# Two of the weight sums of the MLPs' seven products made by GpSimd in halves, the first one issued one unit sooner

## The chip, the core and the metric

The kernel runs on one core of one Trainium2 chip. Its engines are TensorE (PE in the profile; its weight loads are PEld), VectorE (DVE), ScalarE (ACT), GpSimd (POOL) and SyncE (SP, which here only issues DMAs). Each runs its own queue of instructions in order, and semaphores tie the queues together. The metric is the time of one execution on the device, in microseconds (us), as the median of some runs.

## The reference

A trunk of two decoder layers over 256 tokens of width 2048, all in float32. The first layer's mixer is differential attention, the second's multi-head latent attention. Each layer then attends into 256 memory tokens and ends with an MLP whose hidden width is 8192:

```python
def sq_relu_mlp(h, wup, wdown):
    return jnp.square(jax.nn.relu(h @ wup)) @ wdown

x = x + sq_relu_mlp(rms_norm(x, mlp_norm[i]), mlp_wup[i], mlp_wdown[i])
```

The change touches only the product `h @ wup` of the two MLPs: 256 x 2048 times 2048 x 8192.

## The kernel before, in words

**Precision.** A float32 product is made as three products of halves. Activations and weights are each split into a high part (fp32r) and a low part, the rest; TensorE adds high x high, high x low and low x high. For the weights this is done on the fly. A raw tile of 128 x 2048 float32 (1 MB, one "unit" of the weight stream) comes by DMA; for each of its two halves of 1024 columns ScalarE casts the high part (`whi`, L223) and VectorE subtracts to get the low part (`wlo`, L224: raw minus whi, both in SBUF). There are seven raw tiles (pool `wraw`) and four tiles each of whi and wlo (pool `whalf`), so the split can be at most two units ahead of TensorE.

**Weight stream.** `plan` lists the units in the order of use. `take()` hands TensorE the next unit and refills a list of four ready ones through `fill()`. `fill()` pops a job; before it runs that job, it calls the `fetch` of the job behind it, if it has one. So a fetch is issued one unit ahead of its job's split. SyncE's loads and the accumulating DMAs are kept in program order; TensorE's order is written out by hand. The order of the other instructions of VectorE, ScalarE and GpSimd is chosen by a scheduler that works from its own estimates of times and from dependencies.

**Seven products.** The hidden width is taken in eight blocks of 1024. Blocks 1 to 7 are computed by a scheme of seven products in place of eight (class `Seven`): tokens, width and hidden columns are each cut in two, and sums of the quarters of activations and weights are multiplied (p1 to p7). Each product has two units, x = 0 and 1, of 12 matmuls of 512 columns. The order is p1 p1 p5 p5 p6 p3 p6 p3 p2 p7 p2 p7 p4 p4. Wdown units of earlier blocks (24 matmuls each) are woven in behind seven of these: p1(1), p5(1), both p6, both p2, p7(1).

**Weight sums.** For each x a tile `t` holds a running sum. It is loaded with one quarter. Behind p1 a second quarter is added on the way by an accumulating DMA that GpSimd issues (L961); p5 uses that sum. For p6 the quarter in tile `22` is added to `t` by VectorE (`add`, L969), for p2 the quarter in tile `21` likewise (L969 again, called at L1000); the result is p4's weight. p3 uses tile `22`, behind which another accumulating DMA makes it p7's weight. p6's sum is issued in the job itself, right ahead of its split; it must wait until p5 of the same x has split `t`, and until tile `22` has landed. In the first four of the seven blocks `t` for x = 0 lives in a unit of the activations' pool, which the profile shows as `unit`; otherwise it is a raw tile.

Other work that matters here: L616 adds a finished Wdown chunk to the residual (VectorE, one operand in PSUM); L428 splits transposed hidden activations (VectorE, both operands in SBUF); L394 stores planes for a transpose by DMA (issued by GpSimd). Elsewhere GpSimd makes small products and sums for the rotary embedding (L632 to L637) and two gains at the very end (L1896).

Of the kernel before, what the change touches and what calls it, by code (L numbers as in the profile page):

```python
# [15 lines left out]
ALU = mybir.AluOpType  # L16
# [6 lines left out]
CH = 512  # L23
# [31 lines left out]
def trunk(ctx, tc, x, xT, xT0, mem, memT, positions, gcols, gfinal, lam_vecs, consts, W, out):  # L55
    nc = tc.nc
# [20 lines left out]
    def unit():  # L77
        return units.tile([P, 2, 4, S], F32R, tag="unit", name=nm("unit"))
# [99 lines left out]
    def f32(ap):  # L178
        return ap.bitcast(F32)
# [47 lines left out]
    def halves_of(raw, n=4 * CH, pieces=2):  # L227
        split = split_pieces(raw, n, pieces)
        for _ in range(pieces):
            split.next()  # L230
        return split.halves
# [18 lines left out]
    def fill():  # L250
        while len(ready) < AHEAD and plan:
            job = plan.pop(0)
            if plan and hasattr(plan[0], "fetch"):
                plan[0].fetch()
            if callable(job):
                ready.append(job())
            else:
                name, i, width = job
                ready.append(split_weights(W[name][i, :, : 4 * width], width))
# [685 lines left out]
    class Seven:  # L945
# [20 lines left out]

        def job(self, p, x):
            def add(o, q):
                nc.vector.tensor_tensor(o, o, q, ALU.add)  # L969

            loads = {"p1": (("t", x), (0, 1)), "p6": ((22, x), (1, 1)), "p2": ((21, x), (1, 0))}

            def fetch():
                key, (i, j) = loads[p]
                if key not in self.raw:
                    home = f32(unit()).rearrange("p a k t -> p (a k t)") if p == "p1" and x == 0 and self.b < LAST - 2 else None
                    self.raw[key] = self.fetch(i, j, x, home=home)

            def run():
                r = self.raw  # L980
                if p in loads:
                    fetch()
                if p == "p1":
                    o = self.fetch(0, 0, x)
                    self.fetch(0, 0, x, r["t", x])
                elif p == "p5":
                    o = r["t", x]
                elif p == "p6":
                    o = r["t", x]
                    add(o, r[22, x])  # L990
                elif p == "p3":
                    o = r[22, x]
                    split = halves_of(o)
                    self.fetch(0, 1, x, o)
                    return split
                elif p == "p7":
                    o = r.pop((22, x))
                elif p == "p2":
                    o = r.pop((21, x))
                    add(r["t", x], o)  # L1000
                else:
                    o = r.pop(("t", x))
                return halves_of(o)

            if p in loads:
                run.fetch = fetch
            return run
# [997 lines left out]
```

## Time and profile before

| | |
|---|---|
| median of 3 runs | 2160.42 us (2160.02 to 2160.5) |
| the profiled execution's own time | 2159.85 us |
| its span | 2158.1 us |
| TensorE busy | 2147.1 us (99%) |
| VectorE busy | 1733.3 us (80%) |
| ScalarE busy | 1486.7 us (69%) |
| GpSimd busy | 225.4 us (10%) |
| weight sums on VectorE (L969) | 56 times 2.288 us |

The span reaches from the first to the last instruction of the profiled execution; the time holds some 1.75 us more. Busy means that an instruction of the engine was running; for TensorE the ends are modelled. In the answers on groups, the columns are the line, the engine, the operation, out<-in by tile names, the shapes, the count, busy time and the mean of one in ns, and the idle time ahead of it with what ended it. In a timeline, each row has its start, its duration (of several merged rows, from the first start to the last end) and in brackets the idle time ahead. In the table by stretches, busy times stand with the count of instructions, then the granted clock, the DMA engines' share and GB/s.

### The profile page before, as it was taken

Reading aid. Unit: us, or ns where it says so; the run is one execution under the profiler, and the core shown is the slowest. Engines: PE = TensorE matmul, PEld = TensorE weight load, DVE = VectorE, ACT = ScalarE, POOL = GpSimd, SP = SyncE. Lnnn points to the kernel's source line nnn. Section 1 sums busy time; section 2 is a strip of 40 time slices with the busy share of each in tenths; the row PEclk is TensorE's granted clock in tenths of the full one; section 3 lists DMA queues with packets and bytes.
Section 4 is the critical chain, followed back from the end, with each engine's and each line's share of the span. In section 5 each row is a group of like instructions: output and inputs, shape, how many; then the busy total and the mean of one; then the engine's idle time right before and its main releaser. Section 6 shows DMA issues by size and latency. Waiting matters only on the chain.

```text
span 2158.1 us, 27532 instructions
## 1 busy us (share of the span) xinstructions
PE 2147.1 (99%) x10109; PEld 1796.9 (83%) x10109; DVE 1733.3 (80%) x1962; ACT 1486.7 (69%) x1978; POOL 225.4 (10%) x354
## 2 busy tenths in 40 slices
PE   9999999999999999999999999999999999999998
PEld 7888888888888888888889988888888888888887
DVE  6576878788888889788886878778888888888887
ACT  7576656767777777776665765666777777777665
POOL 1123210001000000000000420000000000000001
PEclk9999999999999999999999999999999999999999
DMA  9678796748999999998986464665999999999995
GB/s 386 207 232 282 226 296 220 234 156 267 295 292 259 312 283 254 318 277 265 305 250 217 135 202 159 225 220 179 289 295 290 266 308 285 268 279 309 261 315 146
DMA packets 173944, 553.72 MB, mean 257 GB/s; under 512 B 100464, under 2 KB 100848, under 8 KB 114928
## 3 DMA queue, kind: packets, MB, share of 16 engines
q1 hardware_dynamic: 155136, 445.26, 58.6%
q0 software_dynamic: 18240, 105.92, 23.2%
q8 instruction: 79, 1.29, 0.2%
q10 hardware_dynamic: 432, 0.79, 0.1%
q14 instruction: 57, 0.47, 0.1%
HBM read 505.38 MB, written 24.12 MB: 245 GB/s over the span
## 4 chain that ended last, share of the span: by engine, by line
PE 96%; DVE 2%; DMA 1%; issue 1%; ACT 0%; DVEq 0%; POOLq 0%; POOL 0%
PE mm L172 63%; PE pr L172 28%; PE ax L172 3%; DMA raw<-in_mlp_wup_dram 1%; PE ax L176 1%; DVE wlo L224 1%; PE mm L176 1%; DVE raw L969 0%; DVE x L616 0%; DVE unit L428 0%; ACT whi L223 0%; PE ax L1326 0%; PE pr L176 0%; DVE unit L382 0%; DVE x L1875 0%
## 5 line engine op out<-in xcount | busy, mean ns | idle before, releaser
L224 DVE TENSOR_TENSOR wlo<-raw,whi 128x1024 fp32r<-128x1024 f32 (+3 forms) x930 | 1118.8, 1216 | 321.2 <-ACT whi L223 299.1
L223 ACT CAST whi<-raw 128x1024 fp32r<-128x1024 f32 (+3 forms) x929 | 968.2, 1044 | 541.6 <-PE mm L172 381.1
L172 PE MATMUL mm<-whi,unit 128*128 128x512 f32 (+2 forms) x4000 | 1268.9, 389 | 0.3
L172 PEld LDWEIGHTS mm<-whi,unit 128*128 128x128 f32 x4000 | 749.0, 188 | 148.9 <-DVE unit L382 1.1
L172 PE MATMUL mm<-wlo,unit 128*128 128x512 f32 (+2 forms) x2000 | 773.8, 387 | 0.2
L172 PE MATMUL pr<-whi,unit 128*128 128x512 f32 x1912 | 610.0, 389 | 0.0
L172 PEld LDWEIGHTS mm<-wlo,unit 128*128 128x128 f32 x2000 | 376.3, 188 | 73.6 <-DVE wlo L224 3.2
L172 PEld LDWEIGHTS pr<-whi,unit 128*128 128x128 f32 x1912 | 358.6, 188 | 73.4
L172 PE MATMUL pr<-wlo,unit 128*128 128x512 f32 x956 | 371.8, 389 | 0.4 <-DVE wlo L224 0.4
L172 PEld LDWEIGHTS pr<-wlo,unit 128*128 128x128 f32 x956 | 179.5, 188 | 39.2 <-DVE wlo L224 2.4
L394 POOL DMA_DIRECT2D turned<-planes x84 | 47.6, 567 | 732.2 <-ACT planes L392 706.6
L969 DVE TENSOR_TENSOR raw<-raw,raw 128x2048 f32<-128x2048 f32 x40 | 91.5, 2288 | 9.0 <-DMA raw<-in_mlp_wup_dram 8.8
L616 DVE TENSOR_TENSOR x<-x,mm 128x512 f32<-128x512 f32 x128 | 85.2, 682 | 15.2 <-PE mm L172 15.1
L961 POOL DMA_DIRECT2D raw<-in_mlp_wup_dram x48 | 43.4, 905 | 448.0 <-DVE wlo L224 425.7
L468 POOL TENSOR_TENSOR rs<-rs,mhalf 128x1 f32<-128x1 f32 (+1 forms) x26 | 21.7, 837 | 385.7 <-DVE rs L467 385.6
L224 DVE TENSOR_TENSOR wlo<-unit,whi 128x1024 fp32r<-128x1024 f32 x48 | 57.3, 1221 | 5.3 <-ACT whi L223 4.0
L223 ACT CAST whi<-unit 128x1024 fp32r<-128x1024 f32 x48 | 49.8, 1054 | 9.8 <-PE pr L172 9.8
L392 ACT COPY planes<-p 128x1024 uint16<-128x1024 uint16 x48 | 50.0, 1041 | 0.3
L172 PE MATMUL mm<-unit,whi 128*128 128x256 f32 x256 | 46.7, 284 | 0.0
L462 ACT ACTIVATE junk<-x 128x512 bf16<-128x512 f32 (+1 forms) x57 | 35.3, 619 | 11.0 <-DVE x L1174 5.2
L1539 ACT ACTIVATE p<-p,r 128x512 f32<-128x512 f32 x42 | 30.4, 724 | 15.3 <-DVE p L1044 7.4
L172 PEld LDWEIGHTS mm<-unit,whi 128*128 128x128 f32 x256 | 40.2, 192 | 0.3
(207 smaller groups left out, 1314.3 us busy)
## 6 DMA issues: line engine op xcount, KB each, us to landing
raw<-in_mlp_wdown_dram SPq DMA_DIRECT2D x128, 1024.0 KB, 7.2
raw<-in_mlp_wup_dram SPq DMA_DIRECT2D x120, 1024.0 KB, 7.0
raw<-in_mlp_wup_dram POOLq DMA_DIRECT2D x48, 1024.0 KB, 9.0
raw<-in_da_wqkv_dram SPq DMA_DIRECT2D x45, 1024.0 KB, 8.6
turned<-planes POOLq DMA_DIRECT2D x84, 256.0 KB, 6.1
raw<-in_da_wo_dram SPq DMA_DIRECT2D x16, 1024.0 KB, 8.2
raw<-in_ca_wkv_dram SPq DMA_DIRECT2D x16, 1024.0 KB, 7.6
raw<-in_mlp_wdown_dram POOLq DMA_DIRECT2D x16, 1024.0 KB, 10.2
```

The source lines that it names most:

```text
L172: return nc.tensor.matmul(o, stationary, moving, start=start, stop=stop, skip_group_check=onto)
L176: nc.tensor.transpose(o, src, ident)
L223: nc.scalar.copy(hi, r)
L224: nc.vector.tensor_tensor(lo, r, f32(hi), ALU.subtract)
L392: nc.scalar.copy(planes, src.bitcast(U16).rearrange("p (w s) -> p s w", s=2))
L394: nc.gpsimd.dma_start(there.rearrange("(q s) w -> q s w", s=2), planes)
L462: return nc.scalar.activation(junk[:, : src.shape[1]], src, AF.Square, scale=scale, accum_out=acc)
L468: nc.gpsimd.tensor_tensor(r[:, :n], r[:, :n], mhalf.broadcast_to([P, n]), ALU.pow)
L616: nc.vector.tensor_tensor(xc, xc, ps, ALU.add)
L961: tc.keep_in_program_order(nc.gpsimd.dma_start(onto, src, accum_op=ALU.add))
L969: nc.vector.tensor_tensor(o, o, q, ALU.add)
L1539: nc.scalar.activation(r, src, AF.Relu, scale=rstd[t])
```

## The change

The sum is made by GpSimd, as two instructions of 128 x 1024 rather than one of 128 x 2048. The sum for p6 is issued in `fetch`, one unit ahead of p6's own split; the sum for p2 stays in its job.

```diff
         def job(self, p, x):
             def add(o, q):
-                nc.vector.tensor_tensor(o, o, q, ALU.add)
+                for at in (slice(0, 2 * CH), slice(2 * CH, 4 * CH)):
+                    nc.gpsimd.tensor_tensor(o[:, at], o[:, at], q[:, at], ALU.add)
...
                     self.raw[key] = self.fetch(i, j, x, home=home)
+                    if p == "p6":
+                        add(self.raw["t", x], self.raw[22, x])
...
                 elif p == "p6":
                     o = r["t", x]
-                    add(o, r[22, x])
                 elif p == "p3":
```

## The prediction

> **What bounds the kernel now.** I read the page first: the busy shares, the chain of work that ended last, and the costliest groups; then who waited for whom; then one steady stretch of an MLP.
>
> ```profile
> PE 2147.1 (99%) x10109; PEld 1796.9 (83%) x10109; DVE 1733.3 (80%) x1962; ACT 1486.7 (69%) x1978; POOL 225.4 (10%) x354
> PE 96%; DVE 2%; DMA 1%; issue 1%; ACT 0%; DVEq 0%; POOLq 0%; POOL 0%
> L224 DVE TENSOR_TENSOR wlo<-raw,whi 128x1024 fp32r<-128x1024 f32 (+3 forms) x930 | 1118.8, 1216 | 321.2 <-ACT whi L223 299.1
> L969 DVE TENSOR_TENSOR raw<-raw,raw 128x2048 f32<-128x2048 f32 x40 | 91.5, 2288 | 9.0 <-DMA raw<-in_mlp_wup_dram 8.8
> ```
>
> TensorE is busy 99% of the span and is 96% of the chain. VectorE has 20% idle time, most of it ahead of the low-half subtraction (L224), where it waits for ScalarE. The sums to be moved are L969. Most of them write a raw tile, the rest a unit that serves as one:
>
> ```profile
> L969 DVE TENSOR_TENSOR unit<-unit,raw 128x2048 f32<-128x2048 f32 x16 | 36.6, 2288 | 0.8 <-DMA raw<-in_mlp_wup_dram 0.6
> PEld mm L172 <- DVE wlo L224: 3.2, 8, 0.5
> PEld pr L172 <- DVE wlo L224: 2.4, 5, 0.6
> ```
>
> So there are 56 sums, four in each of 14 blocks (seven per layer), and 128.1 us of VectorE work. The last two rows are the whole stake on the good side: TensorE's weight loads waited 5.6 us for VectorE's low halves in the entire run. More than about 6 us can't be won.
>
> One block of seven products with its woven Wdown items, from 653.80 to 730.00, is my sample; the next one begins where it ends. The chain of waits inside it:
>
> ```profile
> 664.68 5.44 PE mm L172 x24
> 670.12 5.44 PE pr L172 x24
> 675.56 5.44 PE mm L172 x24
> 681.00 2.72 PE pr L172 x12
> 683.73 5.44 PE mm L172 x24
> 689.16 5.44 PE pr L172 x24
> 694.61 5.44 PE mm L172 x24
> 700.04 5.44 PE pr L172 x24
> 705.48 5.44 PE mm L172 x24
> ```
>
> Every piece follows the one before without a gap: 24 matmuls in 5.44 us. A product unit (pr) lasts 2.72 us, a Wdown unit (mm) 5.44. By the order in the code the pieces are: Wdown; p5(0), p5(1); Wdown D1; p6(0); Wdown D2; p3(0), p6(1); Wdown D3; p3(1), p2(0); Wdown D4. Each unit comes in two halves, so I know when TensorE needs each low half: p6(0) at 681.00 and 682.36, and so on. The engines over the block, then L224 alone, then L969 alone:
>
> ```profile
> 653.80:730.00 76.20, 76.20 (x338) 63.10 (x337) 64.02 (x56) 55.81 (x61) 5.87 (x9) 1.00 0.97 292
> 653.80:730.00 76.20, 49.95 (x42) 1.00 0.97 292
> 653.80:730.00 76.20, 9.15 (x4) 1.00 0.97 292
> ```
>
> TensorE 76.20 of 76.20; VectorE 64.02, of which the sums are 9.15 and the subtractions 49.95; GpSimd 5.87.
>
> **What VectorE does around the sums**, in time:
>
> ```profile
> 665.25 2.36 DVE L224 TENSOR_TENSOR wlo<-unit,whi 128x1024 fp32r<-128x1024 f32 x2 [0.67 <-ACT whi L223]
> 667.64 2.29 DVE L969 TENSOR_TENSOR unit<-unit,raw 128x2048 f32<-128x2048 f32 x1
> 669.85 1.22 DVE L224 TENSOR_TENSOR wlo<-raw,whi 128x1024 fp32r<-128x1024 f32 x1
> 670.99 1.28 DVE L616 TENSOR_TENSOR x<-x,mm 128x512 f32<-128x512 f32 x2
> 696.52 2.36 DVE L224 TENSOR_TENSOR wlo<-raw,whi 128x1024 fp32r<-128x1024 f32 x2
> 698.79 1.89 DVE L428 TENSOR_TENSOR unit<-landed,unit 128x512 fp32r<-128x512 f32 x3
> 700.60 2.35 DVE L224 TENSOR_TENSOR wlo<-raw,whi 128x1024 fp32r<-128x1024 f32 x2
> 702.87 0.69 DVE L428 TENSOR_TENSOR unit<-landed,unit 128x512 fp32r<-128x512 f32 x1
> ```
>
> A sum takes 2.2 us of VectorE's order (667.64 to 669.85), a subtraction 1.14 (669.85 to 670.99, done after 1.22), an L616 or L428 0.6. Slack is small: p2(0)'s first low half is done at 700.60 + 1.22 = 701.82 for a need at 702.76. VectorE runs one to four us ahead of TensorE and no more, as it can split only into buffers that TensorE has freed.
>
> **What a half costs on GpSimd.** The trace has no 128x1024 sum there. It has smaller ones:
>
> ```profile
> 194.85 0.32 POOL L636 TENSOR_TENSOR ev<-rope,rope 128x64 f32<-128x64 f32 x1
> 195.14 0.32 POOL L637 TENSOR_TENSOR ev<-rope,rope 128x64 f32<-128x64 f32 x1
> 1242.32 0.45 POOL L633 TENSOR_TENSOR rope<-ev,sin 128x128 f32<-128x128 f32 x1
> 1242.74 0.45 POOL L634 TENSOR_TENSOR rope<-ev,cos 128x128 f32<-128x128 f32 x1
> ```
>
> Start to start 0.29 for 64 columns (0.28 in the following rows of that stretch) and 0.42 for 128: 0.14 per 64 columns, 2.19 ns each. And two of 512 columns beside VectorE's subtractions:
>
> ```profile
> 2093.38 1.23 DVE L224 TENSOR_TENSOR wlo<-raw,whi 128x1024 fp32r<-128x1024 f32 x1 [0.30 <-ACT whi L223]
> 2094.05 1.72 POOL L1896 TENSOR_TENSOR x<-x,unit 128x512 f32<-128x512 f32 x1 [2.25 <-ACT junk L462]
> 2095.01 0.69 DVE L1174 TENSOR_TENSOR x<-x,pr 128x512 f32<-128x512 f32 x1 [0.41 <-PE pr L172]
> 2135.95 1.22 DVE L224 TENSOR_TENSOR wlo<-raw,whi 128x1024 fp32r<-128x1024 f32 x1
> 2136.34 1.99 POOL L1896 TENSOR_TENSOR x<-x,unit 128x512 f32<-128x512 f32 x1 [17.56 <-ACT junk L462]
> 2137.22 2.19 DVE L224 TENSOR_TENSOR wlo<-raw,whi 128x1024 fp32r<-128x1024 f32 x1
> ```
>
> These six rows decide the prediction. Both GpSimd sums end 1.16 us after the subtraction ahead of them ended (2094.61 to 2095.77; 2137.17 to 2138.33), though one had started 0.56 and the other 0.83 before that end: each waited until VectorE was through. Then it is VectorE's turn to wait: the subtraction at 2137.22 takes 2.19 in place of 1.22 and ends 1.08 after GpSimd's end. They do not overlap; they take turns, one for one. L1174, which reads one operand from PSUM, is not held up (0.69, inside GpSimd's 1.72).
>
> Had the subtraction at 2137.22 followed its predecessor at 1.14, it had ended at 2138.31; it ended at 2139.41. A 512-column sum costs VectorE 1.10. With 512 more columns at 2.19 ns a half costs 1.10 + 1.12 = 2.22, and a whole sum 4.4 in place of 2.2. The bounds of a half: 0 where VectorE would have been idle, and 1.99 + 1.12 = 3.11 if the reported span of the slower row were its price. I take 2.2, since it is a difference of ends and not a span.
>
> On these two points the Trainium skill can be set beside the rows. SBUF — State Buffer, "Who interferes with whom", says that a VectorE instruction with two SBUF inputs and a GpSimd instruction that reads SBUF exclude each other, the later one waiting for the earlier one's end; the rows agree (2.19 for 1.22). Perfetto Trace Analysis, "GPSIMD Engine Instruction", advises spacing over the reported span; by the spans (mean 1.85 for 512 columns) a half would come to about 3 us and my sum below would near double.
>
> **The change part by part.** It removes 4 x 2.2 = 8.8 us from VectorE per block. It adds 8 halves on GpSimd, 8 x 2.2 = 17.6 us during which VectorE can't subtract. Net 8.8 us more in the block's turn-taking; VectorE had 76.20 - 64.02 = 12.2 idle, so on average it still fits. TensorE is only delayed where the halves fall in a dense place. I walk through the sample, in its own times. S is TensorE's delay so far; a need is the chain's time plus S.
>
> p6(0)'s sum can start when p5(0) is split, 667.6. Its first half lies in the old sum's place, 667.64 to 669.85: free. The second comes after p5(1)'s first subtraction: 671.0 to 673.2, the L616 pair beside it. p5(1)'s second low half is done at 674.4 for a need at 674.20: S 0.2. D1's first follows, 675.5. p6(1)'s sum now has its tile free (p5(1) split): half to 677.7, D1's second low half 678.9, need 678.28 + S: S 0.6. Half to 681.05, p6(0)'s first low half 682.3, need 681.00 + S: S 1.3. p6(0)'s second 683.4 and D2's first 684.5 are in time. p2(0)'s sum: half to 686.65, D2's second 687.9, need 686.45 + S: S 1.5. Half to 690.0, p3(0)'s first 691.2, need 689.16 + S: S 2.0. Four subtractions in time, to 695.7. p2(1)'s sum: half to 697.9, D3's second 699.1, in time; half to 701.25, p3(1)'s first 702.5, need 700.04 + S: S 2.5. p3(1)'s second 703.6, three L428 1.8, p2(0)'s first 706.6, need 702.76 + S: S 3.8. One more L428, D4's first 709.5, need 705.48 + S: S 4.0. Behind that VectorE has its idle time back and TensorE pays no more.
>
> So 4.0 us per block, and 14 x 4.0 = 56. The profiled execution took 2159.85 (span 2158.1 and 1.75 around it), the median of the runs 2160.42, 0.57 more. 2159.85 + 56 = 2215.9, plus 0.57: **2216 us**.
>
> **The sooner issue and the queues.** p6's sum moves ahead of one unit's split: two casts on ScalarE, two subtractions on VectorE and, for p6(1), p3(0)'s accumulating DMA on GpSimd. The load that it needs is issued there already, so SyncE's queue keeps its order. In GpSimd's queue these accumulating DMAs (and the stores of turned planes, L394) stand behind it:
>
> ```profile
> 686.51 0.88 POOL L961 DMA_DIRECT2D raw<-in_mlp_wup_dram  x1 [21.28 <-DVE wlo L224]
> 699.28 0.89 POOL L961 DMA_DIRECT2D raw<-in_mlp_wup_dram  x1 [11.89 <-DVE wlo L224]
> ```
>
> GpSimd is idle for 21 us and 12 us ahead of the accumulations, so the sums fit in there. Should a sum wait for its operand, the accumulation behind it waits too, and p7, which reads its result some 10 us later. I cost this at nothing; if the cover is gone, it is up to one sum, 4.4 us, per block. The sooner issue itself brings nothing: p6(0)'s sum was made at 667.64 already, 13 us ahead of its need. Halves rather than wholes let the first cast start after one half and hold VectorE 2.2 at a time and not 4.4.
>
> **The rivals.** (1) *The halves fall in idle time.* 12.2 us idle per block against 8.8 net; if the new order of the queues places them well, S is 1 us or less per block: 2161 to 2176, middle 2168. For it: the average. Against: VectorE's rows from 665 to 682 and 687 to 709 leave almost no gap, and that is where the sums' operands come free. (2) *Not slower: the engines do not exclude each other at this size*, or GpSimd yields. Then L969 simply vanishes from VectorE; TensorE recovers its waits, at most 5.6 us, at least nothing: 2155 to 2161. It decides wherever no subtraction beside a GpSimd half exceeds 1.3 us. Against: the six rows. (3) *Worse.* Either VectorE has no slack to give, 14 x 8.8 = 123 us, 2283; or late subtractions free raw tiles late and push loads back in a DMA system that is 97% busy here, or GpSimd's DMAs queue behind sums: one sum more per block, 14 x 8.4 = 118 us, 2278. For it: the share of 0.97, and what SyncE's loads wait for. Against: a slower block needs its bytes more slowly.
>
> ```profile
> SPq L191 <- DVE wlo L224: 1307.0, 289, 15.1
> ```
>
> **How the numbers follow.** Forecast (2176 to 2250) 0.68; rival 1 0.13; rival 2 0.07; rival 3 0.12. The range takes in the upper half of rival 1 and the lower edge of rival 3: 2168 to 2262. A measurement here tells about 0.2% (4.3 us) from no change: faster 0.03, same 0.09 (the rest of rival 2 and the best of rival 1), slower 0.88.
>
> **What would show it.** Subtractions (L224) of 2 to 3.5 us beside GpSimd sums, their median still 1.22; GpSimd sums of 2.3 to 3.6 as reported; VectorE's busy time not falling by 128 us; weight loads waiting for wlo by tens of us, in the seven blocks alone; a block of about 80 us between equal places. Wrong if L224's longest stays near 2.2 and blocks stay at 76.2, or if TensorE waits for raw tiles' landings instead.

## The result, and the profile after

The changed kernel takes 2248.98 us (median; 2248.27 to 2252.08), the kernel before in the same session 2160.46 us. The ratio is 1.0413, 95% interval 1.0399 to 1.0427: 88.5 us slower. The forecast was 2216 us, in a range of 2168 to 2262.

The page of the changed kernel: busy shares, the chain of work that ended last, and the groups that answer to those shown of before. (The sum is now L970; other lines below it have moved by one or two.)

```profile
PE 2175.0 (97%) x10109; PEld 1796.2 (80%) x10109; DVE 1818.4 (81%) x1906; ACT 1487.1 (66%) x1978; POOL 565.7 (25%) x466
PE 79%; DVE 11%; issue 6%; ACT 2%; DMA 1%; POOL 1%; SPq 0%; DVEq 0%; POOLq 0%; ACTq 0%
L224 DVE TENSOR_TENSOR wlo<-raw,whi 128x1024 fp32r<-128x1024 f32 (+3 forms) x930 | 1318.6, 1435 | 336.6 <-ACT whi L223 318.9
L970 POOL TENSOR_TENSOR raw<-raw,raw 128x1024 f32<-128x1024 f32 x80 | 249.9, 3160 | 48.3 <-DMA raw<-in_mlp_wup_dram 33.3
L970 POOL TENSOR_TENSOR unit<-unit,raw 128x1024 f32<-128x1024 f32 x32 | 94.6, 3032 | 28.2 <-DVE wlo L224 16.6
```

VectorE lost 56 instructions and 128 us of sums, and yet its busy time rose from 1733 to 1818 us: the same 930 subtractions now average 1435 ns in place of 1216, because a subtraction that has begun and waits for GpSimd counts as busy (rows of 2 to 6 us below in place of 1.22). The chain, 96% TensorE before, now runs through VectorE for 11% and through "issue" (time for which the profile shows no other wait) for 6%. Who waited for whom in the changed kernel (total us, times, longest us):

```profile
PEld mm L172 <- DVE wlo L224: 59.3, 47, 2.7
PE mm L172 <- DVE wlo L224: 39.8, 39, 2.2
PEld pr L172 <- DVE wlo L224: 38.3, 36, 2.3
PE pr L172 <- DVE wlo L224: 23.8, 25, 1.9
```

The weight loads' waits for low halves grew from 5.6 to 97.6 us. A matmul stalled by its own weight load is in both kinds of row, so they are not to be added.

The sample block lasts from 664.45 to 747.64 here, 83.19 us and not 76.16. All engines over it, then the subtractions, then GpSimd's sums alone:

```profile
664.45:747.64 83.19, 77.91 (x337) 62.61 (x336) 70.74 (x52) 55.78 (x61) 30.64 (x16) 1.00 0.86 264
664.45:747.64 83.19, 65.19 (x42) 1.00 0.86 264
664.45:747.64 83.19, 25.05 (x8) 1.00 0.86 264
```

The same 42 subtractions took 49.95 us in the block before and 65.19 now. The clock is full (1.00), and the DMA engines' share fell from 0.97 to 0.86: neither makes up the 7 us. What happens in the first half of the block, VectorE and GpSimd in time (each its own timeline):

```profile
679.34 2.42 DVE L224 TENSOR_TENSOR wlo<-raw,whi 128x1024 fp32r<-128x1024 f32 x1 [0.91 <-ACT whi L223]
682.88 2.24 DVE L224 TENSOR_TENSOR wlo<-raw,whi 128x1024 fp32r<-128x1024 f32 x1
685.04 3.42 DVE L224 TENSOR_TENSOR wlo<-raw,whi 128x1024 fp32r<-128x1024 f32 x1
```

```profile
680.64 3.40 POOL L970 TENSOR_TENSOR unit<-unit,raw 128x1024 f32<-128x1024 f32 x1
683.98 3.39 POOL L970 TENSOR_TENSOR raw<-raw,raw 128x1024 f32<-128x1024 f32 x1
687.33 3.38 POOL L970 TENSOR_TENSOR raw<-raw,raw 128x1024 f32<-128x1024 f32 x1
```

GpSimd's halves start 3.34 us apart. One subtraction fits between two of them, 1.14 us; a half therefore costs VectorE 2.20 us, and the prediction had 2.2. In the second half of the block it is different, for p2(0)'s sum:

```profile
701.25 5.94 DVE L224 TENSOR_TENSOR wlo<-raw,whi 128x1024 fp32r<-128x1024 f32 x1 [1.54 <-ACT whi L223]
```

```profile
700.41 0.90 POOL L961 DMA_DIRECT2D raw<-in_mlp_wup_dram  x1 [9.69 <-issue]
701.03 5.06 POOL L970 TENSOR_TENSOR unit<-unit,raw 128x1024 f32<-128x1024 f32 x2
```

Here the subtraction waits out both halves (5.94 us): GpSimd did not give VectorE its turn in between. The chain of waits through the block, at the places where TensorE stands still:

```profile
679.34 2.42 DVE wlo L224
...
682.95 4.84 DVE wlo L224 x2
687.79 0.59 issue
688.38 3.43 DVE wlo L224
...
701.25 2.75 DVE wlo L224
704.00 2.65 issue
...
707.11 4.07 DVE wlo L224 x2
711.17 0.41 issue
711.58 3.43 DVE wlo L224
```

From the start of one matmul to the next it is 0.23 us as a rule. Five matmuls of the block start much later, each the first of its half that reads wlo: by 1.85 us at 688.51 (D1's first half), 0.47 at 691.85 (D1's second), 1.66 at 707.24 (p6(1)'s first), 1.63 at 711.72 and 0.48 at 715.05 (D3's halves). The first two lie beside p6's sums, the other three beside p2's. With 0.10 at 685.17 and about 0.11 us lost at the matmul right behind each of the six they make 6.8 of the 7.0 us.

Late in each MLP something comes on top that the sample doesn't have. In five stretches of some 3.5 us, each beside a stand-still of 2.0 to 2.4 us, the granted clock of TensorE is 0.5 (0.51 from 891.7 to 895.2, ahead of it 2.34 us lost at 890.80), and up to eight matmuls take 0.2 us longer each. By these matmuls it is about 7 of the 92 us that the profiled execution lost. The kernel before has no such stretch ahead of its last 5 us.

### The profile page after: what moved, and what is told of

The parts are those of the page before. It is cut to its first block, busy times and chain, and to the rows that moved or that the text cites. A ratio compares the mean times of both kernels' runs of the same rounds, so it can differ in the third digit from the quotient of the medians.

```text
span 2250.2 us, 27691 instructions
## 1 busy us (share of the span) xinstructions
PE 2175.0 (97%) x10109; PEld 1796.2 (80%) x10109; DVE 1818.4 (81%) x1906; ACT 1487.1 (66%) x1978; POOL 565.7 (25%) x466
## 4 chain that ended last, share of the span: by engine, by line
PE 79%; DVE 11%; issue 6%; ACT 2%; DMA 1%; POOL 1%; SPq 0%; DVEq 0%; POOLq 0%; ACTq 0%
PE mm L172 55%; PE pr L172 20%; DVE wlo L224 10%; PE ax L172 3%; ACT whi L223 2%; PE ax L176 1%; DMA raw<-in_mlp_wup_dram 1%; PE mm L176 1%; DVE x L616 0%; POOL raw L970 0%; DMA raw<-in_xT_dram 0%; DVE unit L428 0%; ACT unit L427 0%; DVE unit L382 0%; ACT planes L392 0%
## 5 line engine op out<-in xcount | busy, mean ns | idle before, releaser
L224 DVE TENSOR_TENSOR wlo<-raw,whi 128x1024 fp32r<-128x1024 f32 (+3 forms) x930 | 1318.6, 1435 | 336.6 <-ACT whi L223 318.9
L970 POOL TENSOR_TENSOR raw<-raw,raw 128x1024 f32<-128x1024 f32 x80 | 249.9, 3160 | 48.3 <-DMA raw<-in_mlp_wup_dram 33.3
L394 POOL DMA_DIRECT2D turned<-planes x84 | 47.8, 570 | 685.8 <-ACT planes L392 670.5
L970 POOL TENSOR_TENSOR unit<-unit,raw 128x1024 f32<-128x1024 f32 x32 | 94.6, 3032 | 28.2 <-DVE wlo L224 16.6
L616 DVE TENSOR_TENSOR x<-x,mm 128x512 f32<-128x512 f32 x128 | 84.9, 679 | 15.7 <-PE mm L172 15.6
L961 POOL DMA_DIRECT2D raw<-in_mlp_wup_dram x48 | 43.8, 913 | 184.8 <-issue 115.1
L224 DVE TENSOR_TENSOR wlo<-unit,whi 128x1024 fp32r<-128x1024 f32 x48 | 57.2, 1218 | 5.7 <-ACT whi L223 5.5
L223 ACT CAST whi<-unit 128x1024 fp32r<-128x1024 f32 x48 | 49.7, 1051 | 13.1 <-PE pr L172 13.1
L1087 POOL DMA_DIRECT2D raw<-in_mlp_wdown_dram x16 | 14.0, 878 | 169.3 <-DVE wlo L224 116.2
```

Source lines behind the costliest of these rows:

```text
L223: nc.scalar.copy(hi, r)
L224: nc.vector.tensor_tensor(lo, r, f32(hi), ALU.subtract)
L394: nc.gpsimd.dma_start(there.rearrange("(q s) w -> q s w", s=2), planes)
L616: nc.vector.tensor_tensor(xc, xc, ps, ALU.add)
L961: tc.keep_in_program_order(nc.gpsimd.dma_start(onto, src, accum_op=ALU.add))
L970: nc.gpsimd.tensor_tensor(o[:, at], o[:, at], q[:, at], ALU.add)
```

## The experiments

**The two sums apart.** First p6's sums alone on GpSimd (p2's go back to VectorE):

```diff
                 elif p == "p2":
                     o = r.pop((21, x))
-                    add(r["t", x], o)
+                    nc.vector.tensor_tensor(r["t", x], r["t", x], o, ALU.add)
```

> Only p6's sums go to GpSimd, in halves and one unit sooner; p2's stay with VectorE. Theory (turns): VectorE's subtractions and GpSimd's sums exclude each other, so each GpSimd half costs VectorE 2.2 us where VectorE has work. In the changed kernel's sample block TensorE lost 1.85 + 0.47 us beside p6's sums and 1.66 + 1.63 + 0.48 us beside p2's. So this run should lose 14 x 2.3 to 2.6 us: 2193 to 2200 us. Rival (late sums: TensorE waits because a sum on GpSimd takes 4.7 us and not 2.3): p6's sums are the only ones read soon after they are made, so nearly all of the 88 us would stay: above 2235 us.

Measured: 2195.42 us, ratio 1.0162 [1.0147, 1.0177]. Blocks of the sample's kind take 78.98 us, 2.8 more than before. Then p2's alone (p6's again in their job, on VectorE):

```diff
                     self.raw[key] = self.fetch(i, j, x, home=home)
-                    if p == "p6":
-                        add(self.raw["t", x], self.raw[22, x])
...
                     o = r["t", x]
+                    nc.vector.tensor_tensor(o, o, r[22, x], ALU.add)
```

> Only p2's sums go to GpSimd, in halves; p6's stay with VectorE in their job. Theory (turns): 14 x 3.8 to 4.4 us over before: 2213 to 2222 us, and with the run that moves p6 alone the two losses add up to about the whole 88 us. Rival (late sums): p2's sums are read only by p4, some 20 us later, so this run should be at 2160 to 2165 us.

Measured: 2209.89 us, ratio 1.0228 [1.0212, 1.0243]; blocks of 80.06 us. The two losses, 35.2 and 49.7 us, add up to 84.9 of the 88.5. The larger belongs to sums that nothing reads for some 30 us (in this run one ends at 696.28, and the next cast of its tile starts at 731.28). So it is not that sums come too late; what they do to VectorE meanwhile costs the time.

**Is it the reading?** GpSimd keeps its place in the queue and the tile it writes, but reads nothing:

```diff
                 for at in (slice(0, 2 * CH), slice(2 * CH, 4 * CH)):
-                    nc.gpsimd.tensor_tensor(o[:, at], o[:, at], q[:, at], ALU.add)
+                    nc.gpsimd.memset(o[:, at], 0.5)
```

> The sums are left out: in each one's place GpSimd writes a constant over the same half of the same tile, at the same point of its queue, without reading SBUF. Theory (turns over the reading of SBUF): the subtractions are not held up; none over 2.2 us in the MLPs, time 2155 to 2162 us. Rival (any work of GpSimd on SBUF holds VectorE up): subtractions beside these writes take over 2 us, time above 2180 us. Rival (queue order: DMAs that GpSimd issues stand behind the sums): also slower than before by as long as the writes last, with TensorE waiting for raw tiles and not for low halves.

Measured: 2156.17 us, ratio 0.9981 [0.9971, 0.9991]. One of these writes and the subtraction beside it, and all subtractions of that run (least, median, most, in ns):

```profile
692.03 0.96 POOL L970 MEMSET raw<- 128x1024 f32 x1 [1.76 <-DVE wlo L224]
```

```profile
692.07 1.23 DVE L224 TENSOR_TENSOR wlo<-raw,whi 128x1024 fp32r<-128x1024 f32 x1
```

```profile
L224 DVE TENSOR_TENSOR wlo<-raw,whi x930: 685/1224/2183, 5.4 to 2140.1; 128x1024 fp32r<-128x1024 f32 x180, 128x768 fp32r<-128x768 f32 x3, 128x640 fp32r<-128x640 f32 x2, 128x512 fp32r<-128x512 f32 x1
```

The subtraction runs through the whole write and is not longer for it; the most, 2183, is the one beside the gain at the very end, as before. GpSimd's queue still holds 112 instructions in these places, behind waits for VectorE. The reading of SBUF is gone, and the whole loss with it. (The wait for the second operand's landing is gone too, and a write, at 0.96 us, is shorter than a half of a sum; but the subtraction that began 0.04 us behind the write was not held up even for these 0.96 us.) On this rule (SBUF — State Buffer, "Who interferes with whom", in the Trainium skill: against two SBUF inputs of VectorE only a GpSimd instruction that reads contends) the trace agrees: 2.2 us per half with reading, none without.

**What could be won at most.** From the kernel before:

```diff
             def add(o, q):
-                nc.vector.tensor_tensor(o, o, q, ALU.add)
+                pass
```

> The sums are left out altogether, on both engines. This is what taking 128 us off VectorE can bring at most. Theory: TensorE sets the pace, and its weight loads waited 5.6 us for low halves in the whole run before: 2154 to 2160 us. Rival (VectorE's load matters in other ways, for instance by freeing raw tiles sooner): below 2150 us.

Measured: 2156.02 us, ratio 0.9981 [0.9972, 0.999]. The sums cost the kernel before 4.2 us in all. However they were moved, no more was there.

**The sooner issue.** The changed kernel, with p6's sum in its job again:

```diff
-                    if p == "p6":
-                        add(self.raw["t", x], self.raw[22, x])
...
                     o = r["t", x]
+                    add(o, r[22, x])
```

> The changed kernel with p6's sum issued in its own job again, not one unit sooner; still on GpSimd in halves. Theory (turns): the sum still needs 4 turns per pair, so the loss stays: 2235 to 2260 us; if the scheduler puts the sum closer to its use it may be some us more. Rival (the sooner issue is what hurts, by putting p6's sums beside p5's subtractions): under 2215 us.

Measured: 2249.17 us, ratio 1.0412 [1.0398, 1.0426]: the changed kernel's own time. And the sooner issue alone, with all sums whole and on VectorE:

```diff
-                for at in (slice(0, 2 * CH), slice(2 * CH, 4 * CH)):
-                    nc.gpsimd.tensor_tensor(o[:, at], o[:, at], q[:, at], ALU.add)
+                nc.vector.tensor_tensor(o, o, q, ALU.add)
```

> All sums on VectorE as whole tiles as before; only p6's are issued one unit sooner. Theory: VectorE made them some 13 us ahead of their use already, so the time stays: 2157 to 2164 us. Rival (the sooner issue is a gain or loss of its own): outside 2156 to 2165 us.

Measured: 2160.07 us, ratio 0.9999 [0.999, 1.0008]. The sooner issue is worth nothing on either engine, and the traces say why: in the sample block it moves no sum. Counted from the start of that block, p6's two sums start at 12.92 and 19.53 us in the changed kernel and at 12.93 and 19.54 with the sum in its job; on VectorE at 14.01 and 21.96 with the sooner issue and at 14.00 and 21.95 before. (Over both MLPs, 100 of the 112 halves and 52 of the 56 whole sums start within one matmul of the same place.) The scheduler had put them as early as that already. What a sum that really runs sooner would bring was therefore not tried.

**The size of a turn.** One GpSimd instruction per sum, and four:

```diff
-                for at in (slice(0, 2 * CH), slice(2 * CH, 4 * CH)):
-                    nc.gpsimd.tensor_tensor(o[:, at], o[:, at], q[:, at], ALU.add)
+                nc.gpsimd.tensor_tensor(o, o, q, ALU.add)
```

> The changed kernel with each sum as one GpSimd instruction of 128x2048. Theory (turns): the same time on the shared reads, but in holds of some 4.6 us against 1 to 4 us of slack: longest subtractions about 5.8 us in many places, 2250 to 2285 us. Rival (halves let a half of p6(1)'s sum start before p5(1) is wholly split and so take a turn too early): 2225 to 2245 us.

Measured: 2277.15 us, ratio 1.0538 [1.0524, 1.0553].

```diff
-                for at in (slice(0, 2 * CH), slice(2 * CH, 4 * CH)):
+                for at in (slice(k * CH, (k + 1) * CH) for k in range(4)):
```

> The changed kernel with each sum in four GpSimd instructions of 128x512. Theory (turns, one for one): a turn costs VectorE 1.1 us and not 2.2, so less of it passes the slack at any one place, the total being the same: 2215 to 2245 us, longest subtraction about 2.4 us where turns alternate. Where GpSimd keeps the reads over several instructions in a row (as it did for both halves of p2(0)'s sum in ten of the fourteen blocks): subtractions of about 6 us there again, four quarters in a row.

Measured: 2228.91 us (2222.55 to 2232.39), ratio 1.0314 [1.03, 1.0329]. With the same sums made by the same engine, the loss is 117, 88.5 and 68 us for turns of 4.4, 2.2 and 1.1. That a smaller turn passes the slack by less fits, but the totals don't show it alone. In the sample block the three lose 8.3, 7.0 and 6.2 us, close together; most of what quarters gain lies in the last two of each MLP's five full blocks (85.9 to 77.5 us and 83.0 to 80.8 in the first MLP). Turns of several instructions in a row (below) also fell from ten to four, and the half clock after long stand-stills took, by the slower matmuls, about 15, 7 and 8 us of the three profiled executions. Finer turns do not make it a gain. 139 subtractions of the last run took 2.0 to 2.6 us, one quarter's wait. Its longest stands in this place, beside p2(0)'s and then p2(1)'s sum:

```profile
782.96 7.99 DVE L224 TENSOR_TENSOR wlo<-raw,whi 128x1024 fp32r<-128x1024 f32 x1 [1.00 <-ACT whi L223]
```

```profile
781.52 0.90 POOL L961 DMA_DIRECT2D raw<-in_mlp_wup_dram  x1 [6.38 <-issue]
782.16 5.28 POOL L970 TENSOR_TENSOR unit<-unit,raw 128x512 f32<-128x512 f32 x4
787.14 2.72 POOL L970 TENSOR_TENSOR raw<-raw,raw 128x512 f32<-128x512 f32 x2
```

It sat out six quarters in a row, straight behind the issue of a DMA.

**The turn that GpSimd keeps.** All ten subtractions over 4.6 us in the changed kernel, and all four over 4 us in the run with quarters, stand beside sums that GpSimd began straight behind L961. So the DMA that stands ahead of p2(0)'s sum was taken away (p7's weights lack that quarter):

```diff
                     split = halves_of(o)
-                    self.fetch(0, 1, x, o)
                     return split
```

> The changed kernel with p3's accumulating DMA left out (p7's weights lack that quarter), so that nothing stands right ahead of p2(0)'s sum in GpSimd's queue. In the changed kernel all ten subtractions of over 4.6 us stood beside a sum that GpSimd began straight behind that DMA's issue. Theory (GpSimd keeps the shared reads over both halves only when it goes into them straight from issuing a DMA): no subtraction over 3.6 us; p2's part of the loss falls, 2215 to 2238 us. Rival (it keeps them whenever VectorE asks early in the first half, whatever stands ahead): subtractions of 5 to 6 us remain, 2240 to 2250 us.

Measured: 2225.63 us, ratio 1.0299 [1.0284, 1.0315]; blocks of 80.84 us in place of 83.2. The row of its subtractions:

```profile
L224 DVE TENSOR_TENSOR wlo<-raw,whi x930: 684/1224/3452, 5.5 to 2209.7; 128x1024 fp32r<-128x1024 f32 x180, 128x768 fp32r<-128x768 f32 x3, 128x640 fp32r<-128x640 f32 x2, 128x512 fp32r<-128x512 f32 x1
```

None waits for two halves any more. The run also takes a load off the DMA system and lets p2's sums start at other moments, so how much of the 23 us is the kept turn alone stays open. In its sample block p2(0)'s sum starts at 691.25, right behind p6(0)'s split, and TensorE loses 0.7 us beside it; D3's halves lose 0.28 and 0.48.

The other traces say when GpSimd keeps its turn. Over the changed kernel and the seven runs with GpSimd sums in parts, a sum began straight behind a DMA's issue while no subtraction was under way 36 times, and each time the next subtraction waited out every part (34 times behind L961, twice behind the store L394, in the run with p6's back half pinned first: 5.39 us). It began with no issue right ahead and no subtraction under way 22 times, a subtraction following within its first part, and each time GpSimd gave way after that part. And 18 times it began straight behind an issue while a subtraction was under way; none of these led to a long hold. So it takes both, the issue right ahead and a VectorE that is not subtracting at that moment.

**Where p6's sums hurt.** In the changed kernel and in the run that moves p6 alone, p6(1)'s first half took its turn ahead of D1's first subtraction. A sum's front half needs only that the front half of `t` has been split. Based on the run that moves p6 alone, the back half is made first:

```diff
-                for at in (slice(0, 2 * CH), slice(2 * CH, 4 * CH)):
+                for at in (slice(2 * CH, 4 * CH), slice(0, 2 * CH)):
```

> As the run that moves p6's sums alone (2195.42 us), but each sum's back half (columns 1024 and up) is made first. Theory (the step of the prediction that failed for p6): a sum's front half needs only that the front half of t has been split for p5, so p6(1)'s first GpSimd half took its turn before D1's first subtraction, which has 1.1 us of slack, and not behind it. With the back half first it must wait for p5(1)'s second subtraction and D1's first goes ahead: the 2.84 us lost per block fall to the 1.3 us of the prediction's walk, 2175 to 2187 us. Rival (the order of the halves does not matter, the number of turns does): 2193 to 2198 us.

Measured: 2195.85 us, ratio 1.0167 [1.0154, 1.0181]. This told nothing on the theory: the scheduler, free to order the two, had put the front half in front again (the sum's own instructions and waits were those of the earlier run). With the order pinned:

```diff
-                    nc.gpsimd.tensor_tensor(o[:, at], o[:, at], q[:, at], ALU.add)
+                    tc.keep_in_program_order(nc.gpsimd.tensor_tensor(o[:, at], o[:, at], q[:, at], ALU.add))
```

> The run with the back half first, once more: there the scheduler had put the front half in front again (its first sum started before p5(0)'s back half was split), so it was a repeat of the run that moves p6 alone. Here the two halves' order is pinned, back half first. Theory: p6(1)'s first turn now falls behind D1's first subtraction; of the 2.84 us lost per block 1.3 to 1.9 remain: 2177 to 2188 us. Rival (only the number of turns counts): 2193 to 2198 us.

Measured: 2182.61 us, ratio 1.0103 [1.0086, 1.012]; blocks of 77.63 us, 1.47 above 76.16. VectorE around D1's first half, in the run that moves p6 alone (p5(1)'s second subtraction, D1's first) and then here (D1's first, D1's second):

```profile
677.99 2.24 DVE L224 TENSOR_TENSOR wlo<-raw,whi 128x1024 fp32r<-128x1024 f32 x1
680.15 3.41 DVE L224 TENSOR_TENSOR wlo<-raw,whi 128x1024 fp32r<-128x1024 f32 x1
```

```profile
678.39 1.21 DVE L224 TENSOR_TENSOR wlo<-raw,whi 128x1024 fp32r<-128x1024 f32 x1
679.53 3.42 DVE L224 TENSOR_TENSOR wlo<-raw,whi 128x1024 fp32r<-128x1024 f32 x1
```

D1's first subtraction waited 2.2 us (the row at 680.15); here it is through at once (678.39, 1.21), and the wait falls on D1's second. There TensorE loses 0.26 us; at D1's first it had lost 1.82. The same GpSimd turns, p6(1)'s a place later, cost 22 us and not 35. TensorE now stands still at the very three places of the prediction's walk: 0.31 us at p5(1)'s second half, 0.26 at D1's second, 0.49 at p6(0)'s first. The walk had 0.2, 0.4 and 0.7.

**Halves on VectorE.** Sums in their jobs as before, but as two instructions each:

```diff
-                nc.vector.tensor_tensor(o, o, q, ALU.add)
+                for at in (slice(0, 2 * CH), slice(2 * CH, 4 * CH)):
+                    nc.vector.tensor_tensor(o[:, at], o[:, at], q[:, at], ALU.add)
```

> All sums on VectorE, in their jobs as before, but as two halves of 128x1024. Theory: the same work on the same engine, 56 more instructions of some 0.06 us of fixed cost each, all off TensorE's path; a first half lets its cast start 1.1 us sooner where a sum is late: 2157 to 2163 us, with 2156 the least that any version can reach by the run without sums. Rival (more instructions shift VectorE's order enough to cost): above 2165 us.

Measured: 2166.25 us (2164.63 to 2173.74), ratio 1.0031 [1.0022, 1.0041]. A small loss, in the rival's range and not in that of the theory. It too is waiting for low halves: the matmuls that wait for wlo (L224) lose 5.7 us in place of 0.4, nearly all of it in the last full block of each MLP (78.7 us and not 77.0 to 77.3) and behind it. Whether the scheduler's new order or the fixed cost of more instructions makes it is not settled. No version with the sums in it is faster than the kernel before.

## Why the prediction was right, and where its size was off

**The sign and the mechanism** were right: VectorE's subtractions and GpSimd's sums exclude each other, and TensorE pays. The run with writes shows it against the rival in which the engines don't exclude each other; the two runs that move one product's sums alone show it against late sums. What was named as the mark to look for came: subtractions of 2 to 3.5 us (and ten longer ones) with the median at 1224 ns, sums of 2.4 to 3.4 as reported, waits for wlo in tens of us. VectorE's busy time even rose.

**The price of a half**, 2.2 us from differences of ends of two rows, was right: 3.34 us apart less 1.14. By the reported mean of 3.1 us per half the price would have been 40% too high. The Trainium skill's advice to take spacing over the reported span (Perfetto Trace Analysis, "GPSIMD Engine Instruction") holds here: the two halves at 701.03, with no subtraction between them, are reported as 2.7 us each and start 2.35 apart.

**The upside** was right: 5.6 us of waits as the ceiling, 4.2 measured without any sums.

**The sooner issue and the queues** at nothing: right for the sooner issue, which moved no sum of the sample. For the queue it was wrong in one respect that I had not listed. I asked what a sum in GpSimd's queue holds up, and not what stands right ahead of the sum.

**The size was off**: 4.0 us per block forecast, 7.0 measured in the sample, 6.3 over all 14 (88.5 / 14). Three steps of the walk failed.

The first: "p6(1)'s sum now has its tile free (p5(1) split): half to 677.7", behind D1's first subtraction. A half needs half a tile. The sum went one turn sooner and D1's first half lost 1.85 us. The walk's S of 1.3 after p6's sums was 2.8 in the run that moves p6 alone; with the order pinned as the walk had it, 1.5. I made the same step for p2(1) ("half to 697.9" behind D3's first). Its first half began at 707.26, before p6(1)'s second subtraction had ended (708.32), and TensorE lost 1.63 + 0.48 us at D3 where the walk had it in time. That one was not tried apart, and not all of it is this step: without the kept turn ahead of it D3 lost 0.28 + 0.48.

The second: "they take turns, one for one". For p2(0) GpSimd kept its turn through both halves, straight behind the issue of p3's DMA, where the walk had one subtraction in between. TensorE lost 1.66 us there at p6(1)'s first half.

The third: where p2(0)'s sum runs. The walk had it right behind p6(0)'s split and D2's first subtraction, for 0.2 + 0.5 us at D2's second half and p3(0)'s first. In GpSimd's queue it stood behind p3(0)'s accumulating DMA, issued at 700.41, once p3(0) was split; p6(0) had been split by 694.07. So it fell on p6(1). In the run without that DMA it ran behind p6(0)'s split and cost the 0.7 us of the walk.

Against this, the walk's later steps (p3(1), the three L428, p2(0): 0.5 + 1.3 + 0.2) cost nothing: the low halves came in time, TensorE being so much later by then. Of the eight places at which the walk has TensorE pay, only two lost time here: p5(1)'s second half (0.10 us) and D1's second (0.47). That the total came within the range owes something to luck, too much at some places against too little at others. And the half clock after long stand-stills, about 7 us of the profiled execution, was no term of the sum.

**The third rival's** figure for VectorE without slack, 2283 us, is near what whole sums gave (2277). That turns of 4.4 us leave hardly any slack to hide them would fit; but some 15 us of that loss are the half clock, so the agreement may be chance.

## What to carry to other kernels

An elementwise operation moved off a busy VectorE to GpSimd was not off VectorE here, as both read two operands from SBUF: look in the trace for a small case of the two side by side, price it by ends and starts, and count turns against slack place by place, not idle time on average. Cutting an instruction in parts also cuts its waits, so its first part can run sooner than wanted; a scheduler may reorder the parts, and moving an issue in the program need not move it in the queue. And where the engine to be relieved is not what the chain goes through, leave the work out once to see the ceiling before moving it.

## What the runs showed that I had not expected

GpSimd can keep VectorE out over several instructions in a row (5.9 us over two halves, 8.0 us over six quarters) when it goes into them straight from issuing a DMA and no subtraction is under way, though elsewhere they alternate; why is open. In one of the runs (p6 alone, back half pinned first) a sum that began with VectorE idle, but not straight behind such an issue, did yield between its halves to a subtraction that asked 0.83 us after its start:

```profile
672.47 2.65 DVE L224 TENSOR_TENSOR wlo<-raw,whi 128x1024 fp32r<-128x1024 f32 x1 [0.91 <-ACT whi L223]
```

In the changed kernel a subtraction that asked 1.25 us after the start of such a sum (953.48, straight behind the issue) still waited out both halves, 4.92 us. So asking early or late in the first half is not what makes the difference. And the same sums cut in two on VectorE itself cost 0.3%.
